# A fused encoder layer on one core: a new order of products in branch A, loads of branch C one step earlier, three operand sums moved in front of the output product, and banks used in turn at its end

## The chip, the cores and the metric

The kernel runs on one core of a Trainium2 chip. The metric is the device time of one execution in microseconds (us). The core has engines that run side by side, each with its own queue of instructions worked off in order: TensorE (PE: matrix products into PSUM, its weight loads shown as PEld), VectorE (DVE), ScalarE (ACT), GpSimd (POOL) and SyncE (SP), which here issues the DMA transfers. An instruction may wait for a semaphore that another engine raises; everything behind it in its queue then waits too. PSUM, which receives the products, consists of banks; a bank of 128 x 512 numbers takes one product here.

## The reference, cut to what matters

One layer works on 1024 prompt rows and 64 sample rows of width 1024 (together 1088 columns here, since the kernel keeps activations transposed).

```python
h = rmsnorm(x, pre_g) * (1.0 + scale) + shift
z = h @ w_in                                   # gives the inputs of three branches and gates g_a, g_b, g_c, g_m
y_a = pool_mixer(a, ...) * silu(g_a)           # 512 wide
y_b = sgu_mixer(u, v, ...) * silu(g_b)         # 512 wide
y_c = rmsnorm(gla_scan(q, k, v, ...), gla_g) * silu(g_c)   # 1024 wide
gm = sigmoid(g_m)
m = gm[A] * (y_a @ w_oa) + gm[B] * (y_b @ w_ob) + gm[C] * (y_c @ w_oc)
out = m @ w_out
x = x + gate * rmsnorm(out, post_g)
```

The change concerns the three branch projections `y_a @ w_oa`, `y_b @ w_ob`, `y_c @ w_oc` and the output product `m @ w_out`. The sums over windows, the gating unit and the scan lie before them and are not touched.

## The kernel before, in words

**Products.** All numbers are float32. A product of float32 quality is made of three matmuls on split operands: a high part (`hi`, cast by ScalarE) and the rest (`lo`, a subtraction on VectorE); hi x hi, hi x lo and lo x hi are added up in PSUM. So every operand costs one cast and one subtraction before TensorE can use it.

**Units.** The large products use a scheme with seven products where eight would stand (Strassen in Winograd's form): a unit of 256 output rows forms B11, T2, T1, B21, T3, T4 and B22 (`s_unit`). The operands named T are sums of blocks, made on VectorE or GpSimd. Products go to three PSUM tiles of two banks each: a pair that is allotted in turn (`sps`, numbers 79 and 80 in the order of the program, called the paired banks below) and `third`. A unit's results are combined in PSUM and in SBUF: B11 and B21 go to the first paired tile; T2, T3 and T4 follow each other in the second one; T1 and then B22 go to `third`. Between them ScalarE copies B11's result into T2's tile before T2 adds to it (`act.copy(vB, vA)`), copies T2's and T1's results to the tiles `u` and `c22`, and VectorE adds T3's result to `c22` and B22's to `u`. T4 and B22 of a unit are not issued at once but kept in `unfinished`, and `finish_unit` issues them within the next unit, after its B11.

**Stages.** Branch A is the projection with `woa` (two steps of the inner dimension, `nkk` = 2, so 12 matmuls of 272 columns a product); branch B the projection with `wob`, done as plain products (`plain_units`); branch C the projection with `woc` in units with `nkk` = 4 (24 matmuls a product). While branch B runs, `blocks_in` loads the four blocks of branch C's operand from DRAM (`z_yc`, four loads each) and makes their sums and splits (`strassen_b`). `weave` takes steps of the two generators in a fixed ratio. The first unit of branch C loads block 3 itself (`fed`). Each projected block, times its gate, is added to `m`, which lies in DRAM (`z_m`) until the output product.

**The output product.** `out_phase` forms `m @ W_out` once more as seven products per four row blocks (`n` = 0 to 6: B11, B21, T2, T3, T4, T1, B22), with `m` as the stationary operand and quarters of W_out (`wo_load`, `wo_in`) as the moving one. `m_sums(j)` loads the four pieces of `m` of block j and makes the operands T2, T3, T4, T1 and B22 from them, one step per `next`. For j = 3 the pieces are still in SBUF. The sums j = 0 to 2 begin in the steps n = 0 and n = 1. `m_plain` makes the plain operands within the last unit of branch C, whose seven products are walked through with a list of steps (`steps`). `final` reads a finished product: ScalarE squares it for the norm, VectorE multiplies it by the gate into SBUF.

**What sets the order.** The program is written as Python generators. A scheduler places each instruction on its engine by priorities, data and free buffers. `ahead()` raises a priority; `behind()` and `after_main()` hold instructions after the latest matmul. So a changed line moves instructions on several engines, and the order of the finished program tells where they went.

Of the kernel before, what the change touches and what calls it, by code (L numbers as in the profile page):

```python
# [78 lines left out]
def tile_hybrid_pool_sgu_gla_step(  # L79
# [36 lines left out]
    cur = {"chain": (nc.tensor, nc.sync)}  # L116
# [480 lines left out]
    def s_unit(src, c0, Bb, nkk, post, off=0, raw=None, feed=None):  # L597
# [7 lines left out]
        def A(i, j):  # L605
            return raw[j][:, :nkk, i * P : (i + 1) * P]
# [27 lines left out]
        def product(ps, w, name, first):  # L634
            w = w_split(w, nkk)
            for kk in range(nkk):
                step(ps, w, name, kk, first)
# [8 lines left out]
        if feed:  # L646
            assert not unfinished
            ws = [w_split(w, nkk) for w in (A(0, 0), s2, s1)]
            for kk in range(nkk):
                feed(kk)  # L650
                for ps, w, name in zip((pA, pB, pC), ws, ("B11", "T2", "T1")):
                    step(ps, w, name, kk, True)
            feed(nkk)
            p1 = stage("p1", F32)
            act.copy(view(p1), vA)
            yield nkk
            dve.tensor_add(view(u), view(p1), vB)
            act.copy(vB, view(u))
            act.copy(view(c22), vC)
            yield nkk  # L660
            yield nkk
        else:
            product(pA, A(0, 0), "B11", True)
            yield nkk
            yield from finish_unit()
            act.copy(vB, vA)
            product(pB, s2, "T2", False)
            act.copy(view(u), vB)
            yield nkk
            product(pC, s1, "T1", True)  # L670
            act.copy(view(c22), vC)
            yield nkk
# [760 lines left out]
    def blocks_in(z, dst, spots):  # L1433
        for j, where in spots:
            t = [
                [load(z[2 * j + i], p * PC, PC, "y", blk)[:, 0:PC] for p in range(2)]
                for i in range(2)
            ]
            strassen_b(dst, j, t[0], t[1], taker(where))
            yield 1.0  # L1440

    def w_unit(src, c0, nk, alloc=None):

# [145 lines left out]
    def m_sums(j):  # L1589
# [3 lines left out]
        def block(i, p):  # L1593
            if j == 3:
                return fresh[i, p]
            own = spots[i, p] = []
            return m_load(2 * j + i, p, own)
# [2 lines left out]
            give(*spots.pop((i, p), ()))  # L1600

        (b11, b12), (b21, b22) = ([block(i, p) for p in range(2)] for i in range(2))
        dve.tensor_sub(b11, b12, b11)
        t2, spot = take()
        dve.tensor_sub(t2, b22, b11)
# [78 lines left out]
    def out_phase(w, sums):  # L1684
# [72 lines left out]
        for n, name in enumerate(("B11", "B21", "T2", "T3", "T4", "T1", "B22")):  # L1757
            if n < 6:
                nxt = wo_in(n + 1)
            if n == 0:  # L1760
                wo_load(2, range(2))
                next(sums[3])
                wo_load(2, range(2, 4))
                next(sums[0])
            elif n < 5:
                wo_load(n + 2)
            if n == 1:
                next(sums[1])
                next(sums[2])
            if 1 < n < 6:  # L1770
                for g in sums:
                    next(g)
# [6 lines left out]
            for i in range(4):  # L1779
                if n == 0 and i % 2 == 0:  # L1780
                    held.append(spsum())
                if n == 0 and i == 2:
                    m_sample()
                if n == 5 and i == 2:
                    more = spsum()
                if n == 1 or n > 4 and i < 2:
                    ps = third[:, i % 2, :]
                else:
                    ps = (held[i // 2] if n < 5 else more)[:, i % 2, :]
                onto = n in (2, 3, 4, 6) or n == 1 and i > 1  # L1790
                if n == 1 and i > 1:
                    act.copy(ps, held[i // 2][:, i % 2, :])
# [233 lines left out]
        0.08,  # L2026
    )
    last = blocks_in(z_yc, Cb, ((3, c_places[42:56]),))
    idle = c_places[56:]
    msum.append(slot(idle.pop())[:, 0:512].rearrange("p (k n) -> p k n", k=KB))  # L2030

    def fed(j):
# [8 lines left out]
    w = []  # L2041
    steps = (
        lambda: (wo_load(0), w.extend(wo_in(0))), lambda: m_plain(0), lambda: m_plain(1),
        lambda: None, lambda: None, lambda: None, lambda: None,
    )
    whole = chain(units(woc, Cb, 4, 2, (3,)), finish_unit())
    for n, step in zip(("B11", "T2", "T1", "B21", "T3", "T4", "B22"), zip(whole, steps)):
# [75 lines left out]
```

## Time and profile before

| | |
|---|---|
| Median of three runs | 1277.62 us (1274.23 to 1281.95) |
| Profiled execution | 1275.3 us, span of the records 1273.5 us |
| Mean granted TensorE clock | 0.986 |
| TensorE busy | 1199.1 us, 94% of the span, 8962 matmuls |
| VectorE busy | 886.2 us, 70%, 1579 instructions |
| ScalarE busy | 595.0 us, 47% |
| GpSimd busy | 310.8 us, 24% |
| HBM | 124.74 MB read, 54.65 MB written |

Branch A runs from 969 to 1023 us of the span, branch B to about 1077, branch C to 1165, and the output product from 1160 to the end. The times in the rows count from the start of the span. In a timeline a row may merge neighbouring instructions of one kind (x4); the bracket behind a row is the idle time of its engine just before it and what ended that. A wait for several semaphores is put down to the one that came last. The granted clock is a share of full speed, which is 2.4 GHz; the other level is 1.2 GHz, and values between are mixtures over a stretch.

### The profile page before, as it was taken

To read this page: it belongs to the slowest core of one execution; us is meant where nothing else is said; L and a number is where in the kernel's file an instruction comes from. 1 tells how busy PE (TensorE), PEld (TensorE's weight loads), DVE (VectorE), ACT (ScalarE), POOL (GpSimd) and SP (SyncE) were. 2 spreads that over 40 slices of the span, in tenths; PEclk is the share of its full clock that TensorE was granted. 3 is DMA by queue.
4 is the path that set the end of the run, shared out by engine and by line. 5 is a ranking of instruction groups with operands and counts; after the bars stand their busy time and mean duration, and the time that the engine had idled before them with its cause. 6 is when DMAs were issued, how large, how long until landed. Compare 5 with 4: busy or idle time off the path is not lost. (4 is left out here: it accounts for less than half of the span.)

```text
span 1273.5 us, 23610 instructions
## 1 busy us (share of the span) xinstructions
PE 1199.1 (94%) x8962; PEld 1129.0 (89%) x8962; DVE 886.2 (70%) x1579; ACT 595.0 (47%) x1216; POOL 310.8 (24%) x261
## 2 busy tenths in 40 slices
PE   5789999999999999999999999999999999999796
PEld 3189899999899999999999999989988899998575
DVE  6976843647655577786457687875458789768867
ACT  7646633454644434454443345445336433334542
POOL 4560121122301124241024314032122112330001
PEclk9979999999999999999999999999999999999899
DMA  8712523242424114232225544635446679648045
GB/s 281 217 54 86 193 94 111 69 140 73 156 72 135 58 60 128 76 123 62 81 89 185 189 128 149 207 111 161 139 137 199 189 225 319 209 157 284 4 141 190
DMA packets 137120, 180.95 MB, mean 142 GB/s; under 512 B 17673, under 2 KB 81215, under 8 KB 137006
## 3 DMA queue, kind: packets, MB, share of 16 engines
q1 hardware_dynamic: 137006, 179.44, 43.9%
q8 instruction: 70, 1.15, 0.4%
q14 instruction: 44, 0.36, 0.1%
HBM read 124.74 MB, written 54.65 MB: 141 GB/s over the span
## 5 line engine op out<-in xcount | busy, mean ns | idle before, releaser
L70 PE MATMUL sps<-h,hi 128*128 128x272 f32 x3344 | 583.3, 294 | 10.2 <-ACT sps L70 4.2
L70 PEld LDWEIGHTS sps<-h,hi 128*128 128x128 f32 x3344 | 479.8, 190 | 18.5 <-ACT sps L70 6.0
L70 PE MATMUL sps<-h,lo 128*128 128x272 f32 x1672 | 354.1, 291 | 0.0
L70 PEld LDWEIGHTS sps<-h,lo 128*128 128x128 f32 x1672 | 265.1, 189 | 1.5 <-issue 0.9
L70 PE MATMUL third<-h,hi 128*128 128x272 f32 x1344 | 233.8, 292 | 2.8 <-DVE u L70 2.5
L70 PEld LDWEIGHTS third<-h,hi 128*128 128x128 f32 x1344 | 192.1, 188 | 5.8 <-issue 2.7
L70 DVE TENSOR_TENSOR lo<-sf,hi 128x512 fp32r<-128x512 f32 (+1 forms) x168 | 120.0, 715 | 96.0 <-ACT hi L70 95.9
L70 ACT CAST hi<-sf 128x512 fp32r<-128x512 f32 (+1 forms) x168 | 100.2, 598 | 153.3 <-PE sps L70 112.1
L70 ACT CAST hi<-raw 128x512 fp32r<-128x512 f32 (+1 forms) x134 | 80.1, 598 | 154.9 <-PE sps L70 98.9
L70 PE MATMUL third<-h,lo 128*128 128x272 f32 x672 | 142.5, 291 | 0.6 <-DVE lo L70 0.6
L70 DVE TENSOR_TENSOR lo<-raw,hi 128x512 fp32r<-128x512 f32 (+1 forms) x134 | 94.0, 703 | 63.8 <-ACT hi L70 55.3
L70 POOL TENSOR_TENSOR x<-x,x 128x256 f32<-128x256 f32 (+3 forms) x77 | 80.4, 1053 | 169.6 <-ACT x L70 80.4
L70 POOL TENSOR_TENSOR sf<-raw 128x512 f32<-128x512 f32 (+1 forms) x38 | 50.0, 1314 | 283.9 <-DVE lo L70 206.4
L70 PEld LDWEIGHTS third<-h,lo 128*128 128x128 f32 x672 | 106.0, 188 | 1.4 <-DVE lo L70 0.8
L70 ACT ACTIVATE x<-x 128x512 f32<-128x512 f32 (+2 forms) x104 | 57.3, 566 | 85.7 <-DVE x L70 82.0
L70 POOL TENSOR_TENSOR sf<-raw,sf 128x512 f32<-128x512 f32 (+1 forms) x38 | 49.6, 1307 | 163.2 <-DVE lo L70 159.9
L70 DVE TENSOR_TENSOR x<-x 128x256 f32<-128x256 f32 (+4 forms) x142 | 72.0, 540 | 21.9 <-DMA x<-z_bc 8.8
L70 DVE TENSOR_TENSOR x<-x,x 128x256 f32<-128x256 f32 (+5 forms) x106 | 64.7, 624 | 9.6 <-ACT x L70 9.1
L70 POOL TENSOR_TENSOR sm<-sm,nhalf 128x1 f32<-128x1 f32 (+3 forms) x36 | 27.7, 774 | 171.5 <-DVE sm L70 171.4
L70 PE MATMUL aps<-x,x 128*128 128x256 f32 (+6 forms) x352 | 53.7, 287 | 0.7 <-ACT vt L70 0.6
L70 DVE TENSOR_TENSOR c<-c,sps 128x544 f32<-128x544 f32 x42 | 30.2, 719 | 28.9 <-PE sps L70 28.9
L70 PE MATMUL aps<-x 128*128 128x128 f32 (+2 forms) x496 | 46.2, 246 | 3.3 <-DVE x L70 3.0
(286 smaller groups left out, 1617.3 us busy)
## 6 DMA issues: line engine op xcount, KB each, us to landing
raw<-in_w_in_dram SPq DMA_DIRECT2D x68, 512.0 KB, 4.1
x<-z_gm SPq DMA_DIRECT2D x48, 272.0 KB, 2.8
z_gm<-t SPq DMA_DIRECT2D x24, 272.0 KB, 3.4
h<-in_x_prompt_dram SPq DMA_DIRECT2D x24, 256.0 KB, 5.4
h<-in_ada_w_dram SPq DMA_DIRECT2D x24, 256.0 KB, 4.3
z_m<-t SPq DMA_DIRECT2D x22, 272.0 KB, 4.4
h<-in_w_out_dram SPq DMA_DIRECT2D x20, 256.0 KB, 5.0
x<-z_yc SPq DMA_DIRECT2D x16, 272.0 KB, 4.5
```

Source lines behind the costliest of these rows:

```text
L70: return f(*args, **kw)
```

## The change

There are four edits. In `s_unit`, for units with `nkk` below 4 (branch A only), the previous unit's T4 is now issued before this unit's B11, and both B11 and the previous B22 are held after the latest matmul. In `blocks_in` the generator stops once more between the loads of a block and its sums, and block 3's loads are issued before branch C begins (`next(last)`). In `m_sums` a stop after the loads is added for j below 3, and the calls that begin these three sums move from `out_phase` to the last unit of branch C, into its steps B21, T3, T4 and B22. In `out_phase` the products n = 5 and n = 6 use `third` and the paired tile in turn instead of `third` for the row blocks 0 and 1 and the paired tile for 2 and 3.

```diff
@@ s_unit
         else:
-            product(pA, A(0, 0), "B11", True)
+            before = finish_unit()
+            if nkk < 4:
+                yield next(before, 0)
+            with after_main() if nkk < 4 and "main" in cur else ExitStack():
+                product(pA, A(0, 0), "B11", True)
             yield nkk
-            yield from finish_unit()
+            with after_main() if nkk < 4 else ExitStack():
+                for c in before:
+                    yield c
             act.copy(vB, vA)
@@ blocks_in
+            yield 0.5
             strassen_b(dst, j, t[0], t[1], taker(where))
-            yield 1.0
+            yield 0.5
@@ m_sums
+        if j < 3:
+            yield
         dve.tensor_sub(b11, b12, b11)
@@ out_phase
                 wo_load(2, range(2, 4))
-                next(sums[0])
             elif n < 5:
                 wo_load(n + 2)
-            if n == 1:
-                next(sums[1])
-                next(sums[2])
...
-                if n == 5 and i == 2:
+                if n == 5 and i == 0:
                     more = spsum()
-                if n == 1 or n > 4 and i < 2:
+                if n == 1:
                     ps = third[:, i % 2, :]
+                elif n > 4:
+                    ps = (more if i % 2 else third)[:, i // 2, :]
                 else:
-                    ps = (held[i // 2] if n < 5 else more)[:, i % 2, :]
+                    ps = held[i // 2][:, i % 2, :]
@@ before and in the last unit of branch C
     last = blocks_in(z_yc, Cb, ((3, c_places[42:56]),))
+    next(last)
...
-        lambda: None, lambda: None, lambda: None, lambda: None,
+        lambda: next(sums[0]), lambda: (next(sums[0]), next(sums[1])),
+        lambda: (next(sums[1]), next(sums[2])), lambda: next(sums[2]),
```

TensorE in branch A, from the end of the first unit's T3 into the next unit, before. `sps_80` is the second paired tile, `sps_79` the first; a row with a wait opens a product or its part with `lo`.

```order
L70 MATMUL sps_80<-h_11504,lo_11733 128x272 [waits DVE_49]
...
L70 MATMUL third<-h_11513,hi_11803 128x272 [waits Activation_49]
...
L70 MATMUL sps_79<-h_11485,hi_11761 128x272 [waits DVE_49]
...
L70 MATMUL third<-h_11513,lo_11804 128x272 [waits DVE_49]
...
L70 MATMUL sps_80<-h_11509,hi_11783 128x272 [waits DVE_49]
...
L70 MATMUL third<-h_11495,hi_11852 128x272 [waits DVE_49,Activation_49]
...
L70 MATMUL sps_80<-h_11491,hi_11829 128x272 [waits Activation_49]
```

The products are T3, B22 (begun), B11, B22 (the rest), T4, T1 and T2. The same place after the change:

```order
L70 MATMUL sps_80<-h_11504,lo_11733 128x272 [waits DVE_49]
...
L70 MATMUL sps_80<-h_11509,hi_11761 128x272 [waits DVE_49]
...
L70 MATMUL sps_79<-h_11485,hi_11787 128x272 [waits Activation_49]
...
L70 MATMUL third<-h_11513,hi_11803 128x272 [waits Activation_49]
...
L70 MATMUL sps_80<-h_11491,hi_11829 128x272 [waits Activation_49]
...
L70 MATMUL third<-h_11495,hi_11852 128x272 [waits DVE_49]
```

T4 now stands directly behind T3 in `sps_80`, then come B11, B22 whole, T2 and, two products later, T1.

VectorE in the last unit of branch C and the beginning of the output product, before. `lo_` are parts of weights for the last unit, `h_2372` to `h_2376` the pieces and sums of the first T2 sum, `h_2378` its `lo`, `h_2405` and `h_2407` those of the third.

```order
L70 TENSOR_TENSOR lo_2335_13974<-sf_2328_13935,hi_2334_13973 128x512
...
L70 TENSOR_TENSOR h_2372_14074<-h_2373_14076,h_2372_14074 128x544
L70 TENSOR_TENSOR h_2333_13970<-t_2331_13965,h_2332_13969 128x544
...
L70 TENSOR_TENSOR h_2376_14083<-h_2375_14080,h_2372_14074 128x544
L70 TENSOR_TENSOR h_2373_14076<-h_2375_14080,h_2373_14076 128x544
...
L70 TENSOR_TENSOR h_2378_14086<-h_2376_14083,h_2377_14085 128x544
...
L70 TENSOR_TENSOR h_2405_14206<-h_2404_14203,w_2401_14197 128x544
...
L70 TENSOR_TENSOR h_2407_14209<-h_2405_14206,h_2406_14208 128x544
```

After the change (`h_2325` to `h_2332` the first sum, `h_2334` its `lo`, `h_2344` what `h_2333` was; `c22_2283` from `sps1` is the read that frees T4's bank; `w_2398` and `h_2407` are parts of W_out's T2):

```order
L70 TENSOR_TENSOR h_2325_13904<-h_2326_13906,h_2325_13904 128x544
L70 TENSOR_TENSOR lo_2353_14012<-sf_2339_13958,hi_2352_14011 128x512
L70 TENSOR_TENSOR h_2326_13906<-h_2328_13910,h_2326_13906 128x544
...
L70 TENSOR_TENSOR h_2332_13944<-h_2328_13910,h_2325_13904 128x544
L70 TENSOR_TENSOR h_2335_13950<-h_2336_13952,h_2335_13950 128x544
L70 TENSOR_TENSOR c22_2283_13720<-c22_2283_13720,sps1_80 128x544
...
L70 TENSOR_TENSOR h_2334_13947<-h_2332_13944,h_2333_13946 128x544
...
L70 TENSOR_TENSOR h_2344_13993<-t_2342_13988,h_2343_13992 128x544
...
L70 TENSOR_TENSOR w_2398_14188<-w_2396_14184,w_2397_14187 128x512
...
L70 TENSOR_TENSOR h_2407_14209<-h_2405_14205,h_2406_14208 128x512
```

The sums are made among the last unit's weight parts and reads; the last entry that the T2 product needs is now a part of W_out. Counted from `lo_2310` (at 1139.35 us before), `h_2407` is instruction 79 before and 78 after.

VectorE at the end, where it reads the last four products, before and after the change (both halves of a tile carry the tile's name):

```order
L70 TENSOR_TENSOR h_2541_14819<-third_78,h_2340_14020 128x512
...
L70 TENSOR_TENSOR h_2544_14843<-third_78,h_2340_14020 128x512
...
L70 TENSOR_TENSOR x_2547_14867<-sps1_80,h_2340_14020 128x512
...
L70 TENSOR_TENSOR x_2550_14891<-sps1_80,h_2340_14020 128x512
```

```order
L70 TENSOR_TENSOR h_2541_14819<-third_78,h_2361_14065 128x512
...
L70 TENSOR_TENSOR h_2544_14843<-sps1_80,h_2361_14065 128x512
...
L70 TENSOR_TENSOR w_2547_14867<-third_78,h_2361_14065 128x512
...
L70 TENSOR_TENSOR w_2550_14891<-sps1_80,h_2361_14065 128x512
```

The second read is now that of the paired tile's first half. On TensorE the four products keep their sequence of banks: `third`, paired, `third`, paired.

## Rows read from the trace of the kernel before

**Rows 1.** Windows: us; busy of PE, PEld, DVE, ACT, POOL; PEclk, DMA, GB/s.

```profile
969.00:1023.00 54.00, 48.23 (x371) 46.65 (x370) 42.19 (x75) 28.03 (x59) 10.74 (x11) 1.00 0.71 225
...
1036.00:1044.00 8.00, 5.62 (x33) 5.44 (x32) 8.00 (x12) 2.88 (x5) 1.67 (x1) 0.79 0.46 143
...
1165.00:1190.00 25.00, 19.12 (x80) 13.90 (x78) 23.65 (x39) 11.82 (x23) 0.00 (x0) 1.00 0.53 194
1190.00:1203.00 13.00, 9.46 (x31) 7.37 (x32) 9.34 (x15) 5.45 (x11) 0.00 (x0) 0.74 0.00 0
```

**Rows 2.** PE groups in branch A: busy us, mean ns, idle before, releasers.

```profile
L70 PE MATMUL sps<-h,hi 128*128 128x272 f32 x168 | 28.4, 291 | 3.8 <-ACT sps L70 3.8
...
L70 PE MATMUL third<-h,hi 128*128 128x272 f32 x80 | 13.6, 292 | 1.4 <-DVE u L70 1.1 <-ACT hi L70 0.3
L70 PE MATMUL third<-h,lo 128*128 128x272 f32 x38 | 7.9, 290 | 0.6 <-DVE lo L70 0.6
```

**Rows 3.** PE timeline, branch A: start us, us, instruction, [idle before, releaser].

```profile
985.97 0.41 PE L70 MATMUL sps<-h,lo 128*128 128x272 f32 x2
```

**Rows 4.** DVE timeline at the same place.

```profile
986.42 0.72 DVE L70 TENSOR_TENSOR c<-c,sps 128x544 f32<-128x544 f32 x1 [0.45 <-PE sps L70]
```

**Rows 5.** PE timeline, an earlier unit of the first projection.

```profile
695.82 0.78 PE L70 MATMUL sps<-h,hi 128*128 128x272 f32 x4 [1.83 <-DVE c L70]
```

**Rows 6.** PE timeline in branch B.

```profile
1039.42 0.74 PE L70 MATMUL sps<-h,hi 128*128 128x272 f32 x4 [2.38 <-ACT hi L70]
...
1044.03 0.67 PE L70 MATMUL third<-h,hi 128*128 128x272 f32 x4
...
1047.04 0.66 PE L70 MATMUL sps<-h,hi 128*128 128x272 f32 x4
```

**Rows 7.** DVE timeline in branch B.

```profile
1035.56 0.73 DVE L70 TENSOR_TENSOR x<-x,x 128x544 f32<-128x544 f32 x1
...
1036.81 1.83 DVE L70 TENSOR_TENSOR sf<-raw 128x512 f32<-128x512 f32 x1
1038.56 0.71 DVE L70 SCALAR_TENSOR_TENSOR t<-x,sps 128x544 f32<-128x544 f32 x1
```

**Rows 8.** PE timeline, first unit of branch C.

```profile
1086.57 0.65 PE L70 MATMUL sps<-h,hi 128*128 128x272 f32 x3 [0.83 <-DVE h L70]
```

**Rows 9.** DVE groups from 1139 to 1196 us, the costliest.

```profile
L70 DVE TENSOR_TENSOR h<-h,h 128x544 fp32r<-128x544 f32 (+4 forms) x31 | 20.3, 691 | 5.3 <-ACT h L70 3.4 <-DMA h<-in_w_out_dram 1.9
```

**Rows 10.** DVE timeline, last unit of branch C and output product.

```profile
1139.35 0.68 DVE L70 TENSOR_TENSOR lo<-sf,hi 128x512 fp32r<-128x512 f32 x1
...
1148.12 0.73 DVE L70 TENSOR_TENSOR h<-h,h 128x544 fp32r<-128x544 f32 x1 [0.27 <-ACT h L70]
...
1150.55 0.73 DVE L70 TENSOR_TENSOR h<-h,h 128x544 fp32r<-128x544 f32 x1 [1.10 <-ACT h L70]
...
1193.45 3.78 DVE L70 TENSOR_TENSOR h<-h,h 128x512 fp32r<-128x512 f32 x6
```

**Rows 11.** PE timeline, start of the output product.

```profile
1192.99 5.00 PE L70 MATMUL third<-h,h 128*128 128x512 f32 x12 [3.17 <-ACT third L70]
...
1200.16 3.04 PE L70 MATMUL third<-h,h 128*128 128x512 f32 x12 [0.55 <-ACT third L70]
1203.04 2.01 PE L70 MATMUL aps<-h,h 128*128 128x512 f32 x8
```

**Rows 12.** PE timeline at the end.

```profile
1258.42 0.39 PE L70 MATMUL third<-x,h 128*128 128x512 f32 x1
...
1263.59 0.50 PE L70 MATMUL sps<-x,h 128*128 128x512 f32 x1 [2.22 <-DVE x L70]
```

**Rows 13.** DVE timeline at the end.

```profile
1262.13 0.69 DVE L70 TENSOR_TENSOR h<-third,h 128x512 f32<-128x512 f32 x1 [1.07 <-ACT scr L70]
...
1262.85 0.69 DVE L70 TENSOR_TENSOR x<-sps,h 128x512 f32<-128x512 f32 x1
```

**Rows 14.** Page, DMA issues: count, KB each, us to landing.

```profile
h<-in_w_out_dram SPq DMA_DIRECT2D x20, 256.0 KB, 5.0
```

## The prediction

> **What bounds the kernel now.** I read the windows by stage first, then the groups of TensorE's idle time with what released them, then the timelines of TensorE and VectorE at each idle spot. TensorE sets the time nearly everywhere, so a change wins only where TensorE stands still. Four such spots belong to this change. In branch A (969 to 1023 us) TensorE idles 5.8 us: 3.8 in front of products in the paired banks that wait for ScalarE's copy, 1.4 and 0.6 in front of products in `third` [rows 1, 2]. In branch B a gap of 2.38 us is followed by matmuls at the lower clock [rows 1, 6]. Around the start of the output product VectorE is busy 23.65 of 25 us and TensorE 19.12, and from 1190 to 1203 the granted clock is 0.74, a mixture of the 1.2 and 2.4 GHz levels [rows 1]. In front of the last product stands a gap of 2.22 us [rows 12].
>
> **Branch A, products held in another order.** Removed: B11 no longer stands between the parts of the previous unit's B22. T2, which waits for a copy of B11's bank, now has the twelve matmuls of B22 (1.5 us) in front of it, and the copy, whose wait was 3.8 / 4 = 0.95 a time, hides behind them. T1 moves behind B21, so VectorE's addition from `third` has two products of time. That takes away 3.8 + 1.4 + 0.6 = 5.8 us [rows 2]. Added: T4 follows T3 directly in the same bank and must wait until VectorE has read T3's sum, four times (the unit before the branch, units 0 to 2). The price: T3's matmuls end at 985.97 + 0.41 = 986.38, the addition starts at 986.42 and takes 0.72 [rows 3, 4], and TensorE resumes 0.05 after such a read, as the product at 1263.59 does after one that ended at 1263.54 [rows 12, 13]. 0.04 + 0.72 + 0.05 = 0.81, four times 3.2 us. The upper end is a place where VectorE came late to such an addition: 1.83 [rows 5], four times 7.3. VectorE has the same neighbours around these additions as before, so I take the nearer row: 3.2 - 5.8 = **-2.6 us**, with ends at -2.9 and +1.5. What is queued behind the waiting T4 is B11, B22 and so all of the unit: nothing hides this wait.
>
> **Third branch, loads a step ahead.** In the order of SP's queue the block loads move by a few places only, since each still waits for a tile that VectorE frees; the loads of branch B and the stores that they pass do not wait for them. What moves is VectorE's work. The gap at 1039.42 is a bank that VectorE reads late: its read at 1038.56 is queued behind a sum of two loaded tiles at 1035.56 and a weight sum at 1036.81 that took 1.83, where such sums otherwise take 0.7 [rows 7]. Afterwards one instruction that waited for GpSimd (0.6) has left that queue, and the weight sums stand ahead of the tile sum that starts GpSimd's work, so the long one may be short (1.15). The weight load that it needs is issued one place later; I charge 0.5, a guess between nothing and the 1.15. So the gap may fall from 2.38 to about 1.1. The clock behind it: 24 matmuls took 1044.03 - 1039.42 = 4.61 us and the next 24 took 1047.04 - 1044.03 = 3.01, a loss of 1.6 [rows 6]; branch A's gaps left the clock at 1.00 [rows 1], so a gap of 1.1 may do so too. Best -1.3 - 1.6 = -2.9, at the other end +0.8: the first unit of branch C waits once for 0.83 on a split operand [rows 8], other operands are now split just before use, and it could wait twice. I take a third of the best, **-1.0 us**, because the loads themselves are issued no sooner.
>
> **The three T2 sums.** Each is four loads of 272 KB, four subtractions on VectorE and a split (a cast on ScalarE, a subtraction on VectorE). 15 VectorE instructions leave the crowded stretch for the last unit. VectorE's chain from 1139.35 to the lower part of the last T2 sum, the fourth of the six at 1193.45, which ends near 1196.0, is 79 instructions; 5.3 us of it is idle, 3.4 behind ScalarE's casts and 1.9 behind loads of W_out [rows 9, 10]. 56.6 - 5.3 = 51.3 us is work. Afterwards the last operand that the T2 product needs is a weight part, number 78: 50.7 us, at 1190.1 if nothing idles. I leave the first two idle spots, 0.3 and 1.1 [rows 10], and 0.5 for loads: 1192.0. Behind it come two matmuls and two products of twelve, which at the full clock follow each other every 2.9 us (1200.16 to 1203.04 [rows 11]): 0.5 + 5.8 = 6.3. The product in aps that began at 1203.04 would begin at 1198.3, 4.7 sooner. The clock: at 1192.99 twelve matmuls took 5.00 us, at 1200.16 they took 3.04; these 2.0 are in the old time [rows 11]. The new stretch keeps TensorE on many short waits from about 1172 to 1192, so I let it lose these 2.0 again, and 0.7 more: **-4.0 us**. Ends: no idle time and the clock kept, 1190.1 + 6.3 = 1196.4, -6.6; all 5.3 idle and 2.0 of clock, 1190.1 + 5.3 + 6.3 + 2.0 = 1203.7, +0.7. The cover of the moved work is VectorE's idle time in the last unit; queued behind it are the split of B22's weights and the addition that frees T4's bank.
>
> The Trainium skill, "TensorE: Matmul & The Clock Gate", section "A second HAM failure mode: psum-queue depth-cycling", says that frequent short idle spells between groups of matmuls make the clock swing between its two levels. The row at 1192.99 agrees, branch A's gaps with a clock of 1.00 do not; by that rule the first rival below would be the outcome.
>
> **Banks in turn.** For the last two products of W_out the four row blocks now go to `third` and the paired tile in turn instead of two and two. TensorE visits the same banks in the same sequence; what changes is the order in which ScalarE and VectorE read them. Before, the last product (1263.59) waited for the read of the first paired bank (1262.85 to 1263.54). That read was queued behind the one of the second half of `third` (1262.13), whose product ran until 1261.3 (1258.42 and the 2.9 of such a product), though the paired bank was complete when `third` took over at 1258.42 [rows 12, 13]. Such a read starts 0.8 behind its product (1261.3 to 1262.13) and takes 0.7; coming first, it is over at 1258.5 + 1.5 = 1260.0, before the product in `third` is. The gap of 2.22 goes, and nothing is late next but the product itself: **-2.2 us**; at worst 0, if VectorE's last rows end the program instead.
>
> **Sum.** -2.6 - 1.0 - 4.0 - 2.2 = -9.8. The profiled execution took 1275.3 us (a span of 1273.5 and 1.8 around it), 2.3 below the median of 1277.62 and inside the runs' 1274.23 to 1281.95. From it the sum gives 1265.5; from the median, which a new measurement is held against, 1277.6 - 9.8 = **1268**.
>
> **The rivals.**
> 1. The clock stays low for all 26 matmuls behind the T2 sums. A matmul there takes 2.9 / 12 = 0.24 us and twice that at 1.2 GHz: 6.2 us more instead of the 2.7 charged, so the third part gives -0.5 and the total is 1271.3. For it: TensorE gets few matmuls from 1172 to 1192. Against: at 1192.99 the clock came back within one product.
> 2. Branch A's trade is lost: 1.83 us for each T4, as at 695.82, and branch B's gap stays. +1.5 and 0 in place of -2.6 and -1.0: 1272.9. Against: the addition at 986.42 began at once.
> 3. Slower: loads in a circle. The second four loads of W_out's third quarter now stand behind twelve loads of sums in SP's queue, and one waits for a place that VectorE frees while VectorE, in order, waits for a load in front of it. A load of W_out takes 5.0 us to land [rows 14], so an uncovered turn costs 5.0 + 0.6. Two turns: 1190.1 + 11.2 + 6.3 = 1207.6, with 2.0 of clock 6.6 later than now; with the other three parts as forecast (-5.8) the total is +0.8, 1278.4, and with branch A at its bad end 1282.5. It decides once those loads land after about 1179, when VectorE comes to them, 58 instructions of 51.3 / 79 = 0.65 us and 1.9 of idle time behind 1139.35. I expect them at 1177 to 1179: one turn nearly covered, not two.
> 4. Better: the good ends together, -2.9 - 2.9 - 6.6 - 2.2 = -14.6: 1263.
>
> **How the numbers follow.** Forecast 0.58, rival 1 0.14, rival 2 0.12, rival 3 0.07, rival 4 0.09. What a measurement of this kernel can tell from no change is about 0.5%, 6.4 us: faster is below 1271.2, slower above 1284.0. The forecast's own range is 1264 to 1273 and lies below the bound in nine cases of ten (0.52); with rival 4 (0.09) and a third of rival 1 (0.05) that makes 0.66 faster. Slower needs rival 3 with more than one other part at its bad end, or something unseen: 0.04. The rest is 0.30. The range that leaves two in ten out is 1262 to 1276.
>
> **What would show it.** Right: in branch A no wait for ScalarE's copy, and four gaps of about 0.8 us behind VectorE's addition; the gap near 1039 halved, with the clock at 1.00; the aps product some 4 us sooner, counted from the start of the last unit; no gap of 2 us in front of the last product. Wrong: gaps of 1.5 us and more in front of T4; VectorE waiting for W_out between 1170 and 1185; a granted clock below 0.74 behind the T2 product; the last product waiting as before.

## The result and the profile after

The change makes the kernel slower: 1283.38 us (median of 20 runs, 1278.87 to 1288.34) against 1275.86 for the kernel before (20 runs, 1270.74 to 1281.95). The ratio is 1.0059, with a 95% interval from 1.0047 to 1.0071: 7.5 us slower, where 9.8 us faster was forecast.

The profiled execution of the changed kernel took 1286.92 us, 3.5 above its median, with a span of 1285.1 us; that of before had 1273.5. Of these 11.6 us, 1.9 had arisen before 968 us, in code that the change leaves alone, so I compare stage by stage: the start of the same matmul (numbered in TensorE's order) in both traces, at the head and the end of each stage. The last column ends at the last matmul; where the banks are changed, 1.2 more lie behind it. Places in the text are times of the kernel that is named.

| us against the profile of before | branch A (968 to 1030) | branch B (to 1056) | end of B and first units of C (to 1130) | rest (to the last matmul) |
|---|---|---|---|---|
| the change | +2.6 | -3.0 | +8.2 | +0.7 |
| branch A's order alone | +2.7 | -0.1 | +0.2 | -0.6 |
| loads alone | -0.6 | -3.8 | +6.9 | -1.0 |
| T2 sums alone | -0.2 | -2.4 | +1.2 | +1.7 |
| banks alone | -0.7 | -2.6 | +0.7 | -3.6 |

Windows of the changed kernel, with the columns of [rows 1]:

```profile
969.00:1023.00 54.00, 46.42 (x350) 45.56 (x349) 39.99 (x69) 26.51 (x55) 11.15 (x11) 0.94 0.66 205
1036.00:1044.00 8.00, 7.12 (x58) 6.94 (x57) 5.00 (x8) 2.02 (x4) 1.36 (x1) 1.00 0.45 140
...
1092.00:1096.00 4.00, 4.00 (x20) 4.00 (x19) 2.98 (x5) 0.00 (x0) 0.00 (x0) 0.52 0.69 220
...
1190.00:1203.00 13.00, 8.03 (x31) 5.31 (x30) 13.00 (x23) 9.23 (x18) 0.00 (x0) 1.00 0.15 52
1203.00:1218.00 15.00, 12.00 (x37) 8.92 (x37) 6.67 (x12) 5.27 (x12) 0.00 (x0) 0.77 0.00 0
```

In [rows 1] branch A had a granted clock of 1.00 and now has 0.94; branch B rose from 0.79 to 1.00. The dip at 1092 us in branch C's first unit is new. The dip at the start of the output product, 0.74 from 1190 to 1203 us before, now stands behind 1203 us with 0.77.

**Branch A.** TensorE and then VectorE, the changed kernel, where the projection's last unit ends:

```profile
970.54 0.41 PE L70 MATMUL sps<-h,lo 128*128 128x272 f32 x2
975.88 1.27 PE L70 MATMUL sps<-h,hi 128*128 128x272 f32 x4 [4.93 <-DVE c L70]
...
992.32 0.77 PE L70 MATMUL sps<-h,hi 128*128 128x272 f32 x4 [0.88 <-DVE c L70]
```

```profile
969.77 1.88 DVE L70 TENSOR_TENSOR h<-x,h 128x544 fp32r<-128x544 f32 x1
971.58 1.82 DVE L70 TENSOR_TENSOR lo<-sf,hi 128x512 fp32r<-128x512 f32 x1
973.31 1.88 DVE L70 TENSOR_TENSOR h<-T,h 128x544 fp32r<-128x544 f32 x2
975.12 0.70 DVE L70 TENSOR_TENSOR c<-c,sps 128x544 f32<-128x544 f32 x1
```

T3 ends at 970.95 (970.54 + 0.41), and the first T4 waits until 975.88, since the addition that reads T3's sum stands in VectorE's queue behind four splits of branch A's operands and weights. The T4 behind it is slow as well: its first four matmuls take 1.27 us, those of the T4 at 992.32 take 0.77. That T4 waits 0.88, close to the forecast 0.81, and so do the two after it. VectorE's first two rows take over twice the 0.7 of their like. GpSimd works beside them:

```profile
969.35 3.50 POOL L70 TENSOR_TENSOR x<-x,T 128x544 f32<-128x544 f32 x2 [2.96 <-DVE T L70]
```

The Trainium skill, "SBUF — State Buffer", section "Who interferes with whom", says that only the port pair that VectorE and GpSimd share causes contention, as an exclusive lock, and that a VectorE instruction with two inputs in SBUF contends with a GpSimd instruction that reads SBUF. These rows agree: two GpSimd instructions of 1.75 us, and two of VectorE's, with two inputs each, stretched from 0.7 to 1.8 and 1.9.

**Branch C's first unit.** VectorE, then TensorE, the changed kernel:

```profile
1086.89 0.71 DVE L70 TENSOR_TENSOR T<-x,x 128x544 f32<-128x544 f32 x1
1087.52 0.71 DVE L70 TENSOR_TENSOR h<-T,h 128x544 fp32r<-128x544 f32 x1
1088.16 1.87 DVE L70 TENSOR_TENSOR h<-x,h 128x544 fp32r<-128x544 f32 x1
```

```profile
1088.29 0.65 PE L70 MATMUL sps<-h,hi 128*128 128x272 f32 x3 [1.63 <-DVE h L70]
...
1090.08 1.04 PE L70 MATMUL third<-h,hi 128*128 128x272 f32 x3 [0.65 <-DVE h L70]
...
1098.16 0.77 PE L70 MATMUL third<-h,hi 128*128 128x272 f32 x4 [0.97 <-ACT c L70]
```

The split at 1087.52 is that of block 2's T sum; TensorE starts 0.06 behind it, having waited 1.63. In the kernel before the same split ran at 1070.41 (VectorE, before):

```profile
1070.41 1.72 DVE L70 TENSOR_TENSOR h<-T,h 128x544 fp32r<-128x544 f32 x1
```

The clock of 0.52 at 1092 follows these two gaps; the gap at 1098.16 is a copy by ScalarE that TensorE's former order covered. Before, this unit had one wait of 0.83 [rows 8]; in the T2 sums alone and the banks alone, where the code there is that of before, it had two, of 1.8 and 1.2 together.

**Output product.** TensorE, then ScalarE, the changed kernel:

```profile
1205.09 4.50 PE L70 MATMUL third<-h,h 128*128 128x512 f32 x12
1211.75 4.61 PE L70 MATMUL third<-h,h 128*128 128x512 f32 x12 [2.17 <-ACT third L70]
1216.20 2.01 PE L70 MATMUL aps<-h,h 128*128 128x512 f32 x8
```

```profile
1209.68 0.60 ACT L70 ACTIVATE scr<-third 128x512 bf16<-128x512 f32 x1 [5.12 <-PE third L70]
...
1211.13 0.57 ACT L70 COPY third<-sps 128x512 f32<-128x512 f32 x1 [0.76 <-DVE h L70]
```

Third and fourth row block of B21 now follow each other in `third`. Between them stands a turn: ScalarE's square of the one, VectorE's multiplication, ScalarE's copy for the other, 2.17 us in which TensorE has nothing. Before, seven matmuls of T2 stood there and only 0.55 was left [rows 11].

At the end, the 2.22 of [rows 12] is gone; the largest gap left in front of the last two products is the 0.98 that stood as 0.96 before:

```profile
1268.48 1.64 PE L70 MATMUL sps<-x,h 128*128 128x512 f32 x6 [0.98 <-DVE sps L70]
```

### The profile page after: what moved, and what is told of

Its sections match the earlier page's. It is cut to its first block, busy times and chain, and to the rows that moved or that the text cites. A ratio compares the mean times of both kernels' runs of the same rounds, so it can differ in the third digit from the quotient of the medians.

```text
span 1285.1 us, 23620 instructions
## 1 busy us (share of the span) xinstructions
PE 1209.7 (94%) x8962; PEld 1137.0 (88%) x8962; DVE 889.4 (69%) x1579; ACT 596.0 (46%) x1216; POOL 309.3 (24%) x261
## 3 DMA queue, kind: packets, MB, share of 16 engines
q8 instruction: 70, 1.15, 0.4%
## 5 line engine op out<-in xcount | busy, mean ns | idle before, releaser
L70 PEld LDWEIGHTS sps<-h,hi 128*128 128x128 f32 x3344 | 483.0, 191 | 23.1 <-DVE c L70 11.5
L70 DVE TENSOR_TENSOR lo<-sf,hi 128x512 fp32r<-128x512 f32 (+1 forms) x168 | 122.7, 731 | 94.2 <-ACT hi L70 94.0
L70 DVE TENSOR_TENSOR x<-x 128x256 f32<-128x256 f32 (+4 forms) x142 | 74.6, 558 | 22.3 <-DMA x<-z_bc 8.8
L70 DVE TENSOR_TENSOR x<-x,x 128x256 f32<-128x256 f32 (+6 forms) x107 | 64.4, 615 | 9.8 <-ACT x L70 9.3
L70 ACT CAST h<-x 128x544 fp32r<-128x544 f32 (+1 forms) x64 | 39.3, 642 | 38.7 <-DMA x<-z_yc 10.4
L70 DVE TENSOR_TENSOR h<-x,h 128x544 fp32r<-128x544 f32 (+1 forms) x59 | 49.5, 855 | 5.9 <-ACT h L70 5.5
```

Source lines behind the costliest of these rows:

```text
L70: return f(*args, **kw)
```

## The experiments

Each ratio is to the kernel before, run on the same chip; microseconds are the ratio less one, times 1275.6.

| kernel | ratio, 95% interval | us |
|---|---|---|
| branch A's order alone | 1.0046 [1.0028, 1.0063] | +5.9 |
| loads alone | 1.0044 [1.0028, 1.0060] | +5.6 |
| T2 sums alone | 1.0030 [1.0014, 1.0045] | +3.8 |
| banks alone | 0.9988 [0.9973, 1.0002] | -1.5 |
| change without branch A's order | 1.0038 [1.0021, 1.0055] | +4.8 |
| change without loads | 1.0019 [1.0001, 1.0038] | +2.4 |
| change without T2 sums | 1.0057 [1.0037, 1.0077] | +7.3 |
| A: first unit in its old place | 1.0006 [0.9987, 1.0024] | +0.8 |
| A: third order | 0.9975 [0.9954, 0.9996] | -3.2 |
| C: loads really ahead | 1.0064 [1.0041, 1.0087] | +8.2 |
| C: block 2's sums in place | 1.0013 [0.9996, 1.0031] | +1.7 |
| T2 sums and both copies early | 0.9998 [0.9981, 1.0015] | -0.3 |
| both copies early | 0.9998 [0.9980, 1.0016] | -0.3 |
| banks and both copies early | 0.9968 [0.9951, 0.9984] | -4.1 |
| the same and T2 sums | 0.9988 [0.9971, 1.0005] | -1.5 |
| A's third order, banks, both copies | 0.9959 [0.9941, 0.9977] | -5.2 |

**The four parts alone.** Each is its piece of the change's diff and nothing else.

> Only the order of held products in the first projection (branch A) is changed. Theory 1, read from the changed kernel's trace: three of the four T4 waits cost about 0.9 us as forecast, but the first T4, the one of the projection's last unit, waits 4.9 us for VectorE's addition, which is queued there behind the splits of branch A's operands, and the matmuls behind it run at a lower clock; sum +2.7 us. Rival, the term of the prediction: -2.6 us. A second rival: the first T4's wait is late only by chance of one profiled run; then -2.6 as well, and the gap in this profile is under 2 us.

> Only the third branch's loads are moved a step ahead (the loads before the sums, and the last block's loads before branch C). Theory 1, read from the changed kernel's trace: branch B gains 3.0 us, since the gap of 2.4 us in it falls to 0.9 and the clock stays up, but the first unit of branch C loses 8.2 us, since block 2's operands are now split only there, VectorE is late with them and the clock falls; sum +5.2 us. Rival, the term of the prediction: -1.0 us, with branch C's first unit no more than 0.8 us later.

> Only the three T2 sums of the output product are moved into the last unit. Theory 1, read from the changed kernel's trace: VectorE reaches the last T2 weight only about 1 us sooner, and the two products of B21 in third, which formerly had T2 matmuls between them, now follow each other, so the turn through ScalarE, VectorE and ScalarE (2.2 us) is open and the clock falls (3.1 us for the two of them); sum +3.5 us. Rival, the term of the prediction: -4.0 us, the product in aps 4 to 5 us sooner. Second rival: the loss needs the later start that the other parts bring; alone this part gains 1 to 4 us.

> Only the banks of the last two output products are taken in turn. Both theories: the gap of 2.2 us in front of the last product goes; -1.5 to -2.2 us. Rival: VectorE's last rows end the program and nothing is gained, 0 within 0.5.

Three of the four lose, and the banks alone are not told from no change. Branch A's order shows the same first T4, with a gap of 4.92. In its profile branch A is 2.7 longer, less than the 5.9 of the runs (interval 3.6 to 8.0). Its profiled execution had a mean clock of 0.985, its eight runs 0.983 on average, and the 28 runs of the kernel before beside them 0.985. By my estimate from these, 0.002 of 1278 us, the other runs lost 2 to 3 us more to the clock than the profiled one; where, no profile shows. The loads alone lose in branch C's first unit: TensorE waits 1.32 for block 2's split there.

```profile
1083.55 1.05 PE L70 MATMUL sps<-h,hi 128*128 128x272 f32 x3 [1.32 <-DVE h L70]
```

The T2 sums alone lose as well, so their loss doesn't need the other parts. The bank reads come in the forecast order, and the last product starts without a gap (banks alone, VectorE, then TensorE):

```profile
1258.07 0.69 DVE L70 TENSOR_TENSOR h<-sps,h 128x512 f32<-128x512 f32 x1 [0.44 <-ACT scr L70]
...
1260.84 0.69 DVE L70 TENSOR_TENSOR x<-third,h 128x512 f32<-128x512 f32 x1 [0.63 <-ACT scr L70]
```

```profile
1259.87 0.39 PE L70 MATMUL sps<-x,h 128*128 128x512 f32 x1
```

The gap of 2.22 is paid back in part behind the last matmul. VectorE's last rows, before and then banks alone:

```profile
1267.42 0.69 DVE L70 TENSOR_TENSOR x<-sps,h 128x512 f32<-128x512 f32 x1 [0.28 <-ACT scr L70]
...
1269.09 0.75 DVE L70 SCALAR_TENSOR_TENSOR x<-x,sm,w 128x512 f32<-128x512 f32 x1 [0.73 <-POOL sm L70]
```

```profile
1263.61 0.69 DVE L70 TENSOR_TENSOR x<-sps,h 128x512 f32<-128x512 f32 x1 [0.63 <-ACT scr L70]
...
1264.29 0.74 DVE L70 SCALAR_TENSOR_TENSOR x<-x,sm,h 128x512 f32<-128x512 f32 x1
1264.95 0.75 DVE L70 SCALAR_TENSOR_TENSOR h<-h,sm,h 128x512 f32<-128x512 f32 x1
...
1266.49 0.75 DVE L70 SCALAR_TENSOR_TENSOR x<-x,sm,w 128x512 f32<-128x512 f32 x1 [0.73 <-POOL sm L70]
```

Two multiplications of the third row block, which before ran ahead of the last read, now stand behind it, so the last rows start 2.88 us behind that read instead of 1.67. In all eight kernels with the banks in turn the last two products take 2.5 to 2.6 less than in the profile of before, and the stretch behind the last matmul 1.2 to 1.3 more.

These kernels also show that branch B's gap of 2.38 and the low clock behind it [rows 6] are not the same in each execution. In the eleven kernels here whose code there is that of before, the gap is 1.31 to 2.62; from 1034 to 1050 us the clock was 1.00 in eight of them, among them those with 2.51 and 2.62, and 0.89 in three, with gaps of 1.96, 1.99 and 2.32. (In the profile of before it was 0.89 in this window.) Two of them (the last kernel of the table, then banks and both copies early; TensorE's row and the window):

```profile
1036.60 0.74 PE L70 MATMUL sps<-h,hi 128*128 128x272 f32 x4 [2.51 <-ACT hi L70]
1034.00:1050.00 16.00, 13.49 (x108) 13.43 (x108) 15.35 (x22) 3.02 (x6) 3.00 (x2) 1.00 0.72 237
```

```profile
1037.36 0.74 PE L70 MATMUL sps<-h,hi 128*128 128x272 f32 x4 [1.99 <-ACT hi L70]
1034.00:1050.00 16.00, 14.01 (x99) 13.82 (x99) 13.91 (x21) 3.37 (x6) 1.99 (x2) 0.89 0.69 219
```

So a good part of the -3.0 that the change shows in branch B is the low clock that the profile of before happened to have there.

**Branch A with the first unit in its old place.**

```
-            if nkk < 4:
+            if nkk < 4 and c0:
                 yield next(before, 0)
...
-            with after_main() if nkk < 4 else ExitStack():
+            with after_main() if nkk < 4 and c0 else ExitStack():
```

> The new order of held products in branch A, but the unit in front of the branch (the last of the projection) finishes in its old place; only units 0 to 2 have T4 behind T3. Theory 1: the 4.9 us wait and the slow matmuls behind it belong to that one T4, whose addition on VectorE stands behind branch A's operand splits; without it three gaps of 0.88 remain against 5.8 us of gaps before, so -2 us against before and about -5 us against the version with all four. Rival: the new order is itself the cost (all four T4 make TensorE wait and the clock falls somewhere); then the time is not below that of before.

The loss of 5.9 goes, so it hangs on that one T4. But the gain of 2 doesn't come either (the interval goes from a gain of 1.7 to a loss of 3.1). TensorE's rows with a wait, this kernel, and then the waits for ScalarE's copy in the kernel before:

```profile
977.66 0.74 PE L70 MATMUL third<-h,hi 128*128 128x272 f32 x4 [1.15 <-DVE u L70]
981.12 0.77 PE L70 MATMUL sps<-h,hi 128*128 128x272 f32 x4 [1.72 <-ACT sps L70]
986.71 0.78 PE L70 MATMUL sps<-h,hi 128*128 128x272 f32 x4 [0.81 <-DVE c L70]
998.41 0.77 PE L70 MATMUL sps<-h,hi 128*128 128x272 f32 x4 [0.88 <-DVE c L70]
1010.05 0.77 PE L70 MATMUL sps<-h,hi 128*128 128x272 f32 x4 [0.89 <-DVE c L70]
```

```profile
981.59 0.77 PE L70 MATMUL sps<-h,hi 128*128 128x272 f32 x4 [1.26 <-ACT sps L70]
...
993.77 0.77 PE L70 MATMUL sps<-h,hi 128*128 128x272 f32 x4 [0.86 <-ACT sps L70]
...
1017.19 0.77 PE L70 MATMUL sps<-h,hi 128*128 128x272 f32 x4 [0.92 <-ACT sps L70]
```

The T4 waits stand where waits for ScalarE's copy stood (0.86, 0.76 and 0.92 before). Those of the first unit, 1.15 and 1.72 here and 1.15 and 1.26 before, have nothing to do with the order inside the branch.

**Branch A in a third order.**

```
-            product(pA, A(0, 0), "B11", True)
+            inner = nkk < 4 and c0
+            with after_main() if inner else ExitStack():
+                product(pA, A(0, 0), "B11", True)
             yield nkk
-            yield from finish_unit()
+            before = finish_unit()
+            while True:
+                with after_main() if inner else ExitStack():
+                    c = next(before, None)
+                ...
```

> Branch A in a third order, inside the branch only: T3, B11 of the next unit, T4, B22, T2. T4 has B11 between it and the T3 whose sum VectorE must read, T2 has B22 between it and the copy it waits for. Theory 1: the new order of the change trades one wait of ScalarE's copy (0.76 to 0.92 us, three times) for one of VectorE's addition (0.81 to 0.89, three times), one for one; here both are covered, so the three gaps go and branch A is 2.5 us shorter than before, the total -1 to -3 us. Rival: such gaps are not on the path (VectorE's queue sets the pace of the branch), and the total does not move.

Gained: 3.2 us (interval 0.5 to 5.9). TensorE's group of the paired banks in branch A, this kernel, against an idle time of 3.8 in [rows 2]:

```profile
L70 PE MATMUL sps<-h,hi 128*128 128x272 f32 x184 | 31.0, 290 | 2.2 <-ACT sps L70 2.1
```

Two of the three gaps go; one of 0.81 for the copy stays, and so does the first unit's 1.27.

**Branch C's loads really ahead, and block 2's sums in place.** In the changed kernel the half step before the sums moves no load forward: a step of the side work is issued when the credit allows, and the sums now take half a step of it more. What the early `next(last)` does by itself no kernel here shows. The first kernel here loads block j + 1 in front of block j's sums; the second has the change's half step for blocks 0 and 1 alone, and no early `next(last)`.

```
+        t = loads(0)
+        for j, where in spots:
+            n = loads(j + 1)
+            strassen_b(dst, j, t[0], t[1], taker(where))
+            yield 1.0
+            t = n
```

```
-            yield 0.5
+            yield 0.5 if j < 2 else 0.0
             strassen_b(dst, j, t[0], t[1], taker(where))
```

> Branch C's loads really a step ahead: in each step the next block's loads are issued in front of the current block's sums, and the sums stand where they stood before. (In the changed kernel the loads stand where they stood and the sums come half a step later.) Theory 1: the loss of 6 us in branch C's first unit comes from the sums of block 2 that come late, not from loads; here that unit is as before, and the total is between -1 and +1 us. Rival: loads held in the ring of tiles for longer starve the gate loads or the stores of branch B, and branch B is 2 to 5 us longer.

> The half step in front of the sums for blocks 0 and 1 of branch C's operand alone; the sums of block 2 follow their loads at once, as before. Theory 1: the late sums of block 2 are what branch C's first unit lost 6 us by, so that unit is within 1 us of before, and the total -1 to +1 us. Rival: the sums of blocks 0 and 1, which also come later, push VectorE's whole queue back; then the unit stays 4 us or more longer.

The first lost in the way that its rival named, gate loads that come late: branch B shows a new gap of 2.71 us in front of a product that waits for VectorE, which had waited for a gate load, and block 3's splits come late behind another such wait (TensorE, then VectorE, this kernel):

```profile
1057.96 1.28 PE L70 MATMUL sps<-h,hi 128*128 128x272 f32 x4 [2.71 <-DVE t L70]
```

```profile
1057.19 0.72 DVE L70 SCALAR_TENSOR_TENSOR t<-x,sps 128x544 f32<-128x544 f32 x1 [2.45 <-DMA x<-z_gm]
...
1076.37 0.72 DVE L70 SCALAR_TENSOR_TENSOR t<-x,sps 128x544 f32<-128x544 f32 x1 [1.17 <-DMA x<-z_gm]
```

So it says nothing on the sums. The second takes 3.9 of the 5.6 us back (uncertain by 3.0). Its block 2 T sum runs at 1070.60, but in its profile the time from 1056 to 1130 is still 4.5 us longer than before, against 6.9 in the loads alone, with gaps elsewhere:

```profile
1087.89 0.39 PE L70 MATMUL sps<-h,hi 128*128 128x272 f32 x1 [1.54 <-ACT h L70]
```

That wait is for the other split, that of block 3. So the first unit did not come within 1 us of before; it stayed 4 us or more longer, as the rival said, with only the sums of blocks 0 and 1 late. Branch B is 4.1 shorter in the same profile, and the runs lose 1.7 in all (interval -0.5 to 4.0). Late sums of block 2 and late sums of blocks 0 and 1 both cost time in that unit; which cost more isn't settled, since the runs and the profiles divide it differently.

**Both copies early, with and without the T2 sums.**

```
-                if n == 1 and i > 1:
-                    act.copy(ps, held[i // 2][:, i % 2, :])
+                if n == 1 and i == 2:
+                    for h in range(2):
+                        act.copy(third[:, h, :], held[1][:, h, :])
```

> The three T2 sums moved as in the change, and in addition both copies of the held partial sums into third are made ahead of B21's third row block, so that its fourth no longer waits for ScalarE's square, VectorE's product and ScalarE's copy of the third. Theory 1: the 2.2 us turn between the two products and the low clock behind it go, so 2 to 5 us less than the moved sums alone, -1 to +2 us against before. Rival: VectorE's chain up to the last T2 weight sets the time and TensorE only waits elsewhere: within 1 us of the moved sums alone.

> The kernel before with both copies into third made ahead of B21's third row block; the T2 sums stay. In the kernel before, matmuls of T2 stand between the two products and cover the turn, so theory 1 expects little: -1 to 0 us. Rival: the wait of 3.2 us ahead of the third row block and the 2.0 us of low clock belong to the same copies: -2 to -4 us.

By the runs the turn was the price of the moved sums: with both copies early they lose nothing against before (4.1 us less than alone, uncertain by 2.9). TensorE there, moved sums and early copies; the fourth row block starts without a wait:

```profile
1196.37 1.54 PE L70 MATMUL sps<-w,h 128*128 128x512 f32 x6
...
1199.13 2.91 PE L70 MATMUL third<-h,h 128*128 128x512 f32 x12
```

Without the moved sums the copies gain nothing that can be told from the runs. In the profiles the stretch from 1160 to 1203 is 0.7 to 1.7 shorter than before in the three kernels with early copies and without the sums, and as long as before in the two with both. So the turn isn't shown to be the whole price of the sums.

**Combinations, and the change less one part.**

> Banks in turn for the last two products together with both copies into third ahead of B21's third row block; nothing else. By the two profiles apart, the end of the program gains about 3 us and the start of the output product about 2; -3 to -5 us against before. Rival: one wait takes the other's place and only the better of the two remains, -1 to -2 us.

> As the last one, and the three T2 sums moved into the last unit. Theory 1: with the turn in third covered, the moved sums neither win nor lose, since VectorE is busy throughout and only the order of its queue changes: within 1.5 us of the kernel without them. Rival, the term of the prediction: a further -4 us.

> Branch A in the third order (T3, B11, T4, B22, T2), both copies into third ahead of B21's third row block, banks in turn for the last two products. They lie in three stages with other work between them, so theory 1 adds them: -3.2 - 4.1 = -7.3, between -5 and -9 us against before. Rival: TensorE's time won in branch A is given back where VectorE's queue bounds (the start of the output product), -4 us as without it.

> The whole change without its part in branch A (loads, T2 sums and banks remain). If the parts add up as measured alone: 5.6 + 3.8 - 1.5 = +7.9 us against before, and then branch A's part costs nothing within the whole. If branch A costs within the whole what it costs alone (5.9), this is +1.6 us. By the profiles' stages (2.6 to 3.1 us in branch A) I expect +4.5.

> The whole change without the third branch's loads (branch A's order, T2 sums and banks remain). If branch C's part costs within the whole what it costs alone (5.6), this is +1.9 us against before; if the parts add up, 5.9 + 3.8 - 1.5 = +8.2 us. By the profile's stages (branch B -1.4 and branch C +7.7 against the other kernels) I expect +1.5.

> The whole change without the moved T2 sums (branch A's order, loads and banks remain). If the sums cost within the whole what they cost alone (3.8), this is +3.7 us against before; if the parts add up, 5.9 + 5.6 - 1.5 = +10 us. By the stages of the profile (the output product +1.4 with the banks' gain in it, so about 4 for the sums) I expect +4.

Banks and copies together gain 4.1; the T2 sums on top take 2.6 of it away (the intervals overlap), the forecast -4 is excluded. With branch A's third order the kernel is 5.2 us faster than before, the fastest here by its median though not told from the 4.1 without that order; the sum of 7.3 lies just inside its interval (2.9 to 7.5), the rival's 4 too. Leaving parts out shows their cost within the whole: branch A 7.5 - 4.8 = 2.7 us, the loads 7.5 - 2.4 = 5.1, the T2 sums 7.5 - 7.3 = 0.2. Each difference is uncertain by 2.6 to 3.0 us. With the banks' -1.5 they sum to 6.5 of the 7.5; alone they made 13.8. Branch A's loss and that of the T2 sums shrink most, by 3.2 and 3.6 us, each no more than it is uncertain by, so for neither is it shown that it costs less within the whole.

The profiles help here, since each stage is changed in some kernels and left alone in others. The lengths are medians, in us against the profile of before, with the range and the number of kernels:

| part, stretch | with the part | without it | difference |
|---|---|---|---|
| branch A's order, 968 to 1030 | +3.1 (2.6 to 3.6, 4) | -0.6 (-0.7 to -0.2, 10) | +3.6 |
| loads, 1030 to 1056 | -3.4 (-4.1 to -2.1, 4) | -1.7 (-2.6 to -0.1, 11) | -1.8 |
| loads, 1056 to 1130 | +7.5 (6.6 to 8.3, 4) | +0.5 (0.0 to 1.2, 11) | +7.0 |
| T2 sums, copies late, 1160 to 1203 | +2.6 (1.5 to 3.9, 4) | -0.1 (-0.4 to 0.8, 8) | +2.7 |
| banks, 1256 to the last matmul | -2.6 (-2.6 to -2.5, 8) | 0.0 (-0.1 to 1.5, 9) | -2.5 |
| banks, behind the last matmul | +1.2 (1.2 to 1.3, 8) | 0.0 (0.0 to 0.2, 9) | +1.2 |

So the loads do gain some 2 us in branch B and lose 7 in the first units of branch C, the banks gain 1.3 in all, and in the four kernels with the T2 sums and without early copies that stretch is 1.5 to 3.9 longer, most of all in the change itself. These differences add up to 10 us, against 7.5 by the runs (6.0 to 9.1); each comes from one execution of each kernel.

## Why the prediction was wrong

**Branch A, -2.6 forecast; +2.7 within the whole, +5.9 alone, +3.6 by the stages.** Two steps failed. The price of 0.81 for a T4 held three times (0.88). The first of the four cost 4.93 and a spell of low clock, because the prediction said that VectorE has the same neighbours around these additions as before and took the nearer row. The queue was the same, but it mattered only where B22 and B11 no longer stood in front of T4: in the profile of before the same addition came 4.3 us behind T3's last matmul (which ended at 969.07), and TensorE had B11 and B22 to do meanwhile:

```profile
973.34 0.71 DVE L70 TENSOR_TENSOR c<-c,sps 128x544 f32<-128x544 f32 x1
```

And the gain was overcounted: of the 5.8 us, 0.56, 1.15 and 1.26 are waits at the branch's first unit, for a split, for VectorE's addition and for a copy, and they stay (0.55, 1.15, 1.72) with that unit in its old place. So the copy waits that the order could remove were three of 0.86, 0.76 and 0.92, and not four of 0.95; against three T4 waits that is one for one. Rival 2 had its price of 1.83 on all four T4; a higher one fell on one.

**Loads, -1.0 forecast; +5.1 within the whole, +5.6 alone; by the stages -1.8 in branch B and +7.0 behind it.** The step "could wait twice", +0.8 at the other end, was the wrong size: it bounded the waits by the one row of 0.83 and left out that a split moved behind the last covered product delays three products at once, changes TensorE's order, and brings the clock down. The first half was right as far as it goes (gap 0.88, clock 1.00). But its 1.6 for the clock came from one profile, and in eight of eleven kernels with the code of before there the clock did not fall.

**T2 sums, -4.0 forecast; +3.8 alone, 0.2 within the whole by the runs, +2.7 by the stages.** VectorE's chain came out nearly as worked: from its first instruction to the end of the last T2 weight 1139.35 to 1192.0 was forecast, 52.7 us; the T2 sums alone took 1138.93 to 1192.27, 53.3. (Waits for loads were 1.9 there, for the pieces of `m`, where 0.5 was left for them; 0.7 less work made up for half of that.) What failed is the step behind it, "two matmuls and two products of twelve", 6.3 us. These are TensorE's rows in that kernel:

```profile
1194.22 3.03 PE L70 MATMUL third<-h,h 128*128 128x512 f32 x12 [1.16 <-DVE w L70]
1199.41 4.58 PE L70 MATMUL third<-h,h 128*128 128x512 f32 x12 [2.17 <-ACT third L70]
1203.79 2.07 PE L70 MATMUL aps<-h,h 128*128 128x512 f32 x8
```

From 1192.27 to 1203.79 it is 11.5 us. The turn in `third` stands open, because the matmuls that covered it were those whose operands now come sooner. Rival 1's low clock came true in part: twelve matmuls took 4.58, and in the changed kernel 4.50 and 4.61, against 3.04 at full clock; but the eight behind them took 2.07 and 2.01 as before. Rival 3, the circle of loads, did not: in the changed kernel the one wait of VectorE over 0.2 us from 1170 us to the last weight is 0.97, for a cast by ScalarE, none for W_out.

**Banks, -2.2 forecast; -1.5 by the runs (from a gain of 3.4 to a loss of 0.3), -2.5 and +1.2 by the stages.** The reads come in the forecast order and the gap goes. The step that failed is "nothing is late next but the product itself": two multiplications, 1.3 us, that had found room ahead of the last read while the last product came late, are late next, behind that read. The prediction had named VectorE's last rows as its worst case.

**The sum.** The terms were wrong for one reason: each counted a wait of TensorE as gone and looked at the mover's own queue, not at what the moved work or the wait had covered until then.

## What to carry to other kernels

A product between two others is cover: before it is moved, look up what runs late behind it unseen (here an addition that came 4 us late in both kernels), and give a reader and its next writer another product in between rather than trade one wait for another. Where side work is issued by credit, "loads a step ahead" can mean sums a step behind; read which instruction moved. A wait of one profile, and the clock behind it, is a draw: other kernels that leave the stage alone tell how far it varies.

## What the runs showed of the hardware

Gaps of TensorE did not cost the clock alike, and their length alone did not tell. In branch A T4s behind gaps of 0.88 began with four matmuls in 0.77 us, the one behind 4.93 with four in 1.27. At one place in branch B, with the same code, gaps of 2.51 and 2.62 were followed by a clock of 1.00 and gaps of 1.96 and 1.99 by 0.89 (1034 to 1050 us). VectorE's 0.7 us instructions took 1.82 to 1.88 while GpSimd worked; in branch C one of those hit was the last split that TensorE waited for in the changed kernel.
